# A two-layer hybrid decoder trunk on one core: all block sums of the MLP on VectorE, those of the last two channel pairs later, and the norm's sums issued further on

## The chip, the cores and the metric

The kernel runs on one core of a Trainium2 chip. A core has TensorE (PE, matrix products), VectorE (DVE), ScalarE (ACT), GpSimd (POOL) and SyncE (SP, which here only issues transfers). Each engine works through its own queue in order. The metric is the time of one execution in device microseconds, lower is better.

## The reference

Two layers over x of 1024 positions by 1024 channels, in float32. Each layer:

```
h = h + concat(pool_mixer(u), dilated_attention(q, k, v)) @ w_out      # from rmsnorm(h, norm1) @ w_in
hn = rmsnorm(h, norm2)
h = h + square(relu(hn @ w_up)) @ w_down                               # w_up 1024x4096, w_down 4096x1024
h = h + sigmoid(rmsnorm(h, norm3) @ w_gate) * (p[i] @ w_ple)
```

and a last rmsnorm. `rmsnorm(x, g) = x * rsqrt(mean(x*x) + eps) * g`, over the channels.

## The kernel before, in words

Activations are kept with channels on partitions, one tile of 128 channels by 1024 positions. The two products of the MLP are done by a scheme of seven products: the 2x2 block product of a pair of weight tiles with a pair of channel tiles and two halves of the positions takes seven products P1 to P7 of sums of blocks, in place of eight. So sums of blocks are needed on both sides. The sums of weights are made in `Seven.sums` (L305 to L319), four instructions per set of weights: `u0s` and `u1s` for the first product of layer 0 and 1 (w_up), `d0s` and `d1s` for the second (w_down). The sums of the activations that enter the second product are made in `Up.sums` (L1240 to L1263), four instructions `ys` per pair of channel tiles, after relu and square (`y`). Every block or sum that enters a product is split in two parts that TensorE takes at its fast rate: ScalarE makes the high part (L331, L1275), VectorE the rest (L333 for weights `u0p`, `d0p`; L1277 for activations `wP`). Each piece is thus three products of 128x512 for each of 4 channel pairs, 12 in all.

The first product (`Up`) has 16 sets, one per channel pair of the hidden layer; sets 0 and 1 go side by side, as do the last two, 14 and 15. Its results go to DRAM as `x_d`, seven blocks per pair, and come back one piece at a time (`x_back`, L1270). The second product (`Down`) has 16 steps of 7 pieces, 84 products each; a step takes 4 channel pairs into one pair of output tiles. Two steps use the same channel pairs, and it is in the second of the two that blocks for the steps to come are loaded. After a piece, VectorE adds its result into `acc` (L1294), and as P1, P6, P5 and P3 of a set share a bank of PSUM (X), P7 and P4 another (Z), the next piece of that bank begins when `acc` has read the one before.

The second norm's scale is needed at the gating after the first product's pieces (L1232), so its sums (`ss_b`, L469, eight column products that TensorE does in 16 records), its root and its broadcast by TensorE (`rb_b`, L494) are put among the first pieces of the first product. What is summed there, `sq_b`, is added up by GpSimd (L458) from squares that ScalarE makes.

The order of instructions is written by a planner, `Clock`: each strand of work is a generator that yields the ns until its next instruction, and the products move a clock of their own. Every engine's queue is filled in the order in which the clock comes to its strands. Tiles in SBUF are taken in turn from one pool of 49 blocks (`blk`); an instruction that takes a block up waits until the one that used it last has finished.

Before the change, `Seven.sums` runs on GpSimd throughout, and `Up.sums` on VectorE except for the last two pairs, 14 and 15 (`rush`), whose sums run on GpSimd at the start of the second product.

Of the kernel before, what the change touches and what calls it, by code (L numbers as in the profile page):

```python
# [117 lines left out]
def body(nc, tc, pools, A, out):  # L118
# [3 lines left out]
    def blk(name, dt=F32, shape=(128, 1024)):  # L122
        return sb.tile(list(shape), dt, name=name, tag="b")
# [102 lines left out]
    class Seven:  # L226
# [10 lines left out]
        def __init__(self, sets, seq, name, lead=(12, 6, 4), side=0):  # L237
            self.sets, self.seq, self.name = sets, seq, name
            load, sums, make = lead
            self.raw, self.sum, self.piece = {}, {}, {}  # L240
            self.first = {}
            self.begin, t = [], 0.0
            for q, (j, _) in enumerate(seq):
                self.first.setdefault(j, q)
                self.begin.append(t)
                t += 675.0 * sets[j][2]
            self.kicks = []
            for j, q in self.first.items():
                self.kick(q, load, lambda j=j: self.load(j))
                self.kick(q, sums, lambda j=j: ck.go(self.sums(j)))  # L250
            for q, (j, P) in enumerate(seq):
                fn = lambda j=j, P=P: ck.go(self.make(j, P), (name, j, P))
                if q < side:
                    self.kicks.append((-9000.0 + 1200.0 * q, fn))
                else:
                    self.kick(q, make, fn)
            self.kicks.sort(key=lambda x: x[0])
# [47 lines left out]
        def sums(self, j):  # L305
            a11, a12, a21, a22 = (self.block(j, t, k) for t in range(2) for k in range(2))
            n = self.sets[j][2]
            ss = self.two("s", n, (2, n, 128))
            s = [ss[0]()]
            add = nc.gpsimd.tensor_tensor  # L310
            self.sum[j] = s
            add(s[0][:, 0], a11, a21, op=OP.subtract)
            yield 1500.0
            add(s[0][:, 1], a21, a22, op=OP.add)
            yield 1500.0
            s.append(ss[1]())
            add(s[1][:, 0], s[0][:, 1], a11, op=OP.subtract)
            yield 1500.0
            add(s[1][:, 1], a12, s[1][:, 0], op=OP.subtract)  # L319
# [118 lines left out]
    class Norm:  # L438
# [8 lines left out]
        def add(self, src, hf):  # L447
            if self.sq is None:
                self.sq = blk(f"sq_{self.name}")
            if self.first[hf]:  # L450
                self.first[hf] = False
                nc.scalar.activation(self.sq[:, hs(hf)], src, AF.Square)
                self.n[hf] += 1
                return
            t = blk(f"sqt_{self.name}")
            nc.scalar.activation(t[:, :512], src, AF.Square)
            yield 700.0
            nc.gpsimd.tensor_tensor(self.sq[:, hs(hf)], self.sq[:, hs(hf)], t[:, :512], op=OP.add)  # L458
            self.n[hf] += 1
# [56 lines left out]
        def start(self, delay, after=None, sums=None, slack=900.0):  # L516
            def chain():
                yield from self.compact(range(8), sums)
                yield slack
                yield from self.bcast()  # L520
                yield 700.0
                if after:
                    after()
                    yield 2500.0
                self.done()
            ck.go(chain(), delay=delay)
# [96 lines left out]
    def layer(L, hT, norm, tabs):  # L623
# [445 lines left out]
        norm2 = Norm(f"b{L}")  # L1069
# [112 lines left out]
        outs = ws = w = None  # L1182


        norm2.start(17000.0, slack=3000.0)
        norm3 = None
        hg3 = {}
        PLACE = {"P1": 0, "P2": 1, "P3": 2, "P7": 3, "P5": 4, "P6": 5, "P4": 6}
# [16 lines left out]
        class Up(Set):  # L1205
# [34 lines left out]
            def sums(self, y):  # L1240

                d = x_d[self.j].rearrange("a p c -> p a c")
                if y is self.y2:
                    nc.sync.dma_start(out=d[:, 1:3], in_=y.rearrange("p (a c) -> p a c", a=2))
                    return
                nc.sync.dma_start(out=d[:, 0], in_=y[:, :512])
                rush = self.j >= n7 - 2
                if rush:
                    yield 6000.0
                sub = (nc.gpsimd if rush else nc.vector).tensor_tensor  # L1250
                slow = 1800.0 if rush else 700.0
                b11, b12, b21, b22 = y[:, :512], y[:, 512:], self.y2[:, :512], self.y2[:, 512:]
                s = [blk(f"ys{i}", F32, (128, 2, 512)) for i in range(2)]
                sub(s[0][:, 0], b22, b12, op=OP.subtract)
                yield slow
                sub(s[0][:, 1], b12, b11, op=OP.subtract)
                yield slow + 700.0
                sub(s[1][:, 0], b22, s[0][:, 1], op=OP.subtract)
                yield slow
                nc.sync.dma_start(out=d[:, 3:5], in_=s[0])  # L1260
                sub(s[1][:, 1], b21, s[1][:, 0], op=OP.subtract)
                yield 8000.0 if rush else 2000.0
                nc.sync.dma_start(out=d[:, 5:7], in_=s[1])  # L1263

        xw = [{} for _ in range(18)]
# [287 lines left out]
    for L in range(DEPTH):  # L1553
        hT, norm = layer(L, hT, norm, tabs if L == 0 else None)
        tabs = None
# [33 lines left out]
```

## Time and profile before

| | |
|---|---|
| time, median of 3 runs | 2304.93 us (2304.41 to 2306.55) |
| profiled execution | 2304.64 us, span 2302.9 us |
| PE busy | 2254.9 us (98%), 11088 records |
| DVE busy | 1684.2 us (73%) |
| ACT busy | 1012.7 us (44%) |
| POOL busy | 729.4 us (32%) |
| mean granted TensorE clock | 0.991 |

Times in the profile are microseconds from the span's start unless marked ns. A product of 128x512 on TensorE is listed with a length of about 390 ns, but the next one starts before it has ended; what counts is the distance from start to start. In rows that merge instructions (x12), the length is that from the first start to the last end. "idle before" is the time an engine stood still in front of an instruction, with the instruction whose end released it. Line numbers are those of the kernel before.

### The profile page before, as it was taken

What the parts mean: (1) busy time and instruction counts of PE and PEld (TensorE: products, weight loads), DVE (VectorE), ACT (ScalarE), POOL (GpSimd) and SP (SyncE); (2) the same over time, 40 slices, a digit from 0 to 9 for tenths busy, and PEclk for the clock granted to TensorE, in tenths of its full rate; (3) what the DMA queues carried; (4) which work ended last, traced back from release to release, by engine and by line L of the source; (5) the groups of instructions that cost most, each with busy time, mean ns of one, the idle gap of its engine ahead of it and who ended that gap; (6) DMA issues with size and microseconds to landing.
All of it is one profiled execution on the core that took longest, in us unless ns stands there. A gap on an engine that the chain in (4) does not pass through costs nothing.

```text
span 2302.9 us, 30834 instructions
## 1 busy us (share of the span) xinstructions
PE 2254.9 (98%) x11088; PEld 1859.6 (81%) x11088; DVE 1684.2 (73%) x2774; ACT 1012.7 (44%) x2147; POOL 729.4 (32%) x554
## 2 busy tenths in 40 slices
PE   8999999999998999999999999999999989999998
PEld 6887788788886888878887878878888868888888
DVE  7555767777779888896565467687777788888845
ACT  5244543433335344454324355344333453434645
POOL 5111126333335332342121122453332353233322
PEclk9999999999999999999999999999999999999999
DMA  6011143354448645431220122234445675546214
GB/s 183 19 48 20 38 111 99 106 172 154 152 143 286 201 129 174 147 115 46 61 60 19 38 48 73 76 101 151 151 151 165 210 239 150 170 133 179 78 57 136
DMA packets 296369, 275.65 MB, mean 120 GB/s; under 512 B 12476, under 2 KB 224056, under 8 KB 296216
## 3 DMA queue, kind: packets, MB, share of 16 engines
q1 hardware_dynamic: 293624, 270.04, 38.0%
q0 software_dynamic: 2272, 3.61, 0.9%
q8 instruction: 87, 1.43, 0.3%
q14 instruction: 66, 0.54, 0.1%
q10 hardware_dynamic: 320, 0.03, 0.0%
HBM read 200.99 MB, written 72.58 MB: 119 GB/s over the span
## 4 chain that ended last, share of the span: by engine, by line
PE 82%; DVE 9%; ACT 4%; POOL 3%; issue 2%; DMA 1%; SPq 0%; DVEq 0%; ACTq 0%; POOLq 0%
PE X L567 28%; PE Z L567 14%; PE Y L567 6%; PE in L552 5%; PE in L554 5%; PE in L550 5%; PE gt L554 3%; PE gt L552 3%; PE gt L550 2%; PE o L836 2%; PE s L785 2%; DVE wP L1277 1%; POOL res L1102 1%; PE e L817 1%; POOL sq_b L458 1%
## 5 line engine op out<-in xcount | busy, mean ns | idle before, releaser
L1277 DVE TENSOR_TENSOR wP<-wP 128x512 fp32r<-128x512 f32 x252 | 225.9, 920 | 1.7 <-ACT wP L1275 1.7
L567 PE MATMUL X<-wP,d1p 128*128 128x512 f32 x768 | 183.1, 394 | 10.1 <-DVE acc L1294 5.8
L567 PE MATMUL X<-wP,d0p 128*128 128x512 f32 x768 | 183.0, 394 | 10.1 <-DVE acc L1294 4.9
L567 PE MATMUL X<-xP,u0p 128*128 128x512 f32 x768 | 184.7, 393 | 0.0
L567 PE MATMUL X<-xP,u1p 128*128 128x512 f32 x768 | 184.5, 393 | 0.0
L567 PEld LDWEIGHTS X<-wP,d1p 128*128 128x128 f32 x768 | 145.2, 190 | 42.7 <-ACT wP L1275 5.7
L567 PEld LDWEIGHTS X<-wP,d0p 128*128 128x128 f32 x768 | 145.1, 190 | 42.6 <-ACT wP L1275 5.7
L567 PEld LDWEIGHTS X<-xP,u0p 128*128 128x128 f32 x768 | 145.8, 190 | 30.4
L567 PEld LDWEIGHTS X<-xP,u1p 128*128 128x128 f32 x768 | 145.6, 190 | 30.4
L1235 ACT ACTIVATE y<-y 128x1024 f32<-128x1024 f32 x64 | 67.5, 1055 | 219.7 <-DVE y L1232 219.7
L191 DVE SCALAR_TENSOR_TENSOR wl<-wr,gt,wh 128x128 fp32r<-128x128 f32 (+1 forms) x288 | 117.9, 441 | 44.4 <-ACT wh L197 44.1
L1275 ACT ACTIVATE wP<-wP 128x512 fp32r<-128x512 f32 x252 | 146.5, 617 | 3.1 <-DMA wP<-x_d 2.8
L680 POOL TENSOR_TENSOR rot<-rot,s 128x512 f32<-128x512 f32 x48 | 61.7, 1288 | 255.6 <-DVE rot L678 136.7
L804 ACT ACTIVATE sm<-sm,nm 128x128 f32<-128x128 f32 (+1 forms) x192 | 84.2, 440 | 79.9 <-DVE nm L801 77.6
L1294 DVE TENSOR_TENSOR acc<-acc,X 128x512 f32<-128x512 f32 x128 | 86.9, 679 | 35.0 <-PE X L567 34.7
L197 ACT ACTIVATE wh<-wr,gt 128x128 fp32r<-128x128 f32 (+1 forms) x304 | 101.8, 397 | 0.5 <-DMA wr<-in_w_in_dram 0.5
L567 PE MATMUL Z<-wP,d0p 128*128 128x512 f32 x384 | 92.7, 391 | 0.0
L567 PE MATMUL Z<-wP,d1p 128*128 128x512 f32 x384 | 92.4, 391 | 0.0
L567 PE MATMUL Z<-xP,u1p 128*128 128x512 f32 x384 | 91.6, 389 | 0.0
L567 PE MATMUL Z<-xP,u0p 128*128 128x512 f32 x384 | 91.6, 389 | 0.0
L567 PEld LDWEIGHTS Z<-wP,d0p 128*128 128x128 f32 x384 | 72.8, 190 | 15.3
L567 PEld LDWEIGHTS Z<-wP,d1p 128*128 128x128 f32 x384 | 72.6, 189 | 15.2
(478 smaller groups left out, 5864.8 us busy)
## 6 DMA issues: line engine op xcount, KB each, us to landing
wP<-x_d SPq DMA_DIRECT2D x252, 256.0 KB, 3.7
x_d<-ys SPq DMA_DIRECT2D x64, 512.0 KB, 3.7
wr<-in_w_in_dram SPq DMA_DIRECT2D x40, 512.0 KB, 4.7
u0r<-in_w_up_dram SPq DMA_DIRECT2D x32, 512.0 KB, 5.0
x_d<-y SPq DMA_DIRECT2D x32, 512.0 KB, 2.8
u1r<-in_w_up_dram SPq DMA_DIRECT2D x32, 512.0 KB, 5.2
d0r<-in_w_down_dram SPq DMA_DIRECT2D x28, 512.0 KB, 5.7
d1r<-in_w_down_dram SPq DMA_DIRECT2D x28, 512.0 KB, 5.2
```

Source lines behind the costliest of these rows:

```text
L191: nc.vector.scalar_tensor_tensor(l[:, k], raw[:, k], gs[k], f(h[:, k]), op0=OP.mult, op1=OP.subtract)
L197: nc.scalar.activation(h[:, k], raw[:, k], AF.Copy, scale=gs[k])
L550: nc.tensor.matmul(p, wh, h[:, cols], start=first and i == 0, stop=False)
L552: nc.tensor.matmul(p, wh, l[:, cols], start=False, stop=False)
L554: nc.tensor.matmul(p, wl, h[:, cols], start=False, stop=last and i == n - 1)
L567: nc.tensor.matmul(p, w[:, a, i], x[:, b], start=first and i == 0 and a == b == 0, stop=i == n - 1 and a == 1, skip_group_check=not first)
L680: nc.gpsimd.tensor_tensor(a, a, tb["s"][:, hs(hf)], op=OP.mult)
L804: nc.scalar.activation(self.sm[:, p, hh], self.sm[:, p, hh], AF.Exp, bias=nm[:, h:h + 1], scale=0.125, accum_out=ml[g][:, n, 4 + h:5 + h])
L1235: nc.scalar.activation(y, y, AF.Square)
L1275: nc.scalar.activation(t[:, 0], f(t[:, 1]), AF.Copy)
L1277: nc.vector.tensor_tensor(t[:, 1], f(t[:, 1]), f(t[:, 0]), op=OP.subtract)
L1294: nc.vector.tensor_tensor(a, a, p, op=OP.add)
```

## The change

Four edits. The weights' block sums of both products move from GpSimd to VectorE. The activations' block sums of the last two channel pairs move from GpSimd to VectorE too, and start 33000 ns of planned time after their `y` is stored in place of 6000; their own steps are 1500 ns in place of 1800, and the last transfer follows after 6000 in place of 8000. The norm's sums start at 25000 ns of planned time in place of 17000.

```diff
@@ Seven.sums
-            add = nc.gpsimd.tensor_tensor
+            add = nc.vector.tensor_tensor
@@ layer, ahead of the MLP
-        norm2.start(17000.0, slack=3000.0)
+        norm2.start(25000.0, slack=3000.0)
@@ Up.sums
                 rush = self.j >= n7 - 2
                 if rush:
-                    yield 6000.0
-                sub = (nc.gpsimd if rush else nc.vector).tensor_tensor
-                slow = 1800.0 if rush else 700.0
+                    yield 33000.0
+                sub = nc.vector.tensor_tensor
+                slow = 1500.0 if rush else 700.0
...
                 sub(s[1][:, 1], b21, s[1][:, 0], op=OP.subtract)
-                yield 8000.0 if rush else 2000.0
+                yield 6000.0 if rush else 2000.0
                 nc.sync.dma_start(out=d[:, 5:7], in_=s[1])
```

How the order of instructions moves, at three places. First TensorE's queue at the start of the first product of layer 0; `X_3762` and `X_3763` are the banks of sets 0 and 1, `xP` the activations' pieces, `ss_b` the norm's sums. Before the change it reads:

```order
L567 MATMUL X_3762<-xP_3620,u0p 128x512 x3
L567 MATMUL X_3762<-xP_3828,u0p 128x512
L469 MATMUL ss_b_3926<-one,sq_b_3153 128x1 x8
L567 MATMUL X_3762<-xP_3828,u0p 128x512 x2
L567 MATMUL X_3763<-xP_3282,u0p 128x512 x3
```

Now the norm's sums have these rows around them:

```order
L567 MATMUL X_3763<-xP_3455,u0p 128x512 x3
L567 MATMUL X_3763<-xP_3627,u0p 128x512 x3
L567 MATMUL X_3763<-xP_3864,u0p 128x512
L469 MATMUL ss_b_3984<-one,sq_b_3153 128x1 x8
L567 MATMUL X_3763<-xP_3864,u0p 128x512 x2
L567 MATMUL Z_3860<-xP_3303,u0p 128x512 x3
```

The sums stand 36 products further on, near the end of the fifth piece of sets 0 and 1 (P5) in place of inside the fourth (P6); `rb_b` follows 27 products behind them, as against 27 before.

Second, VectorE's queue at the start of the second product of layer 0, around the first `acc`; `d0r` are raw weights, `d0s` their sums, `d0p` the split pieces. Before the change it reads:

```order
L1277 TENSOR_TENSOR wP_6098<-wP_6098 128x512
L1294 TENSOR_TENSOR acc_0_6039<-acc_0_6039,X_6149 128x512
L333 TENSOR_TENSOR d0p<-d0r_5964,d0p 128x512
L1277 TENSOR_TENSOR wP_6111<-wP_6111 128x512
L1277 TENSOR_TENSOR wP_6126<-wP_6126 128x512
```

Now the first `acc` has these rows around it:

```order
L314 TENSOR_TENSOR d0s_6145<-d0r_6088 128x512
L1277 TENSOR_TENSOR wP_6098<-wP_6098 128x512
L1294 TENSOR_TENSOR acc_0_6039<-acc_0_6039,X_6149 128x512
L317 TENSOR_TENSOR d0s_6182<-d0s_6145,d0r_6086 128x512
L333 TENSOR_TENSOR d0p<-d0r_5964,d0p 128x512
L1277 TENSOR_TENSOR wP_6111<-wP_6111 128x512
L319 TENSOR_TENSOR d0s_6182<-d0r_6086,d0s_6182 128x512
L1277 TENSOR_TENSOR wP_6126<-wP_6126 128x512
```

The sums of the next step's weights come between the pieces of this one. From the `y<-y,Y` that stands at 698.91 in the trace up to the first `acc` of the second step's first piece there are 55 instructions before and 63 now.

Third, VectorE's queue from the second into the third step; `ys` are the sums of pairs 14 and 15, made of `y`, and `acc_0_6399` belongs to the third step. Now it reads:

```order
L1294 TENSOR_TENSOR acc_0_6251<-acc_0_6251,X_6298 128x512
L1256 TENSOR_TENSOR ys_6442<-y_5817 128x512
L333 TENSOR_TENSOR d0p<-d0s_6339,d0p 128x512
L1277 TENSOR_TENSOR wP_6393<-wP_6393 128x512
L1254 TENSOR_TENSOR ys_6471<-y_5888,y_5840 128x512
L1277 TENSOR_TENSOR wP_6397<-wP_6397 128x512
L1258 TENSOR_TENSOR ys_6443<-y_5865,ys_6442 128x512
L1294 TENSOR_TENSOR acc_0_6399<-acc_0_6399,X_6458 128x512
L312 TENSOR_TENSOR d0s_6484<-d0r_6403,d0r_6405 128x512
```

Before the change, between the same two `acc`:

```order
L1294 TENSOR_TENSOR acc_0_6258<-acc_0_6258,X_6312 128x512
L333 TENSOR_TENSOR d0p<-d0s_6354,d0p 128x512
L1277 TENSOR_TENSOR wP_6409<-wP_6409 128x512
L1277 TENSOR_TENSOR wP_6413<-wP_6413 128x512
L1294 TENSOR_TENSOR acc_0_6415<-acc_0_6415,X_6471 128x512
```

Three `ys` come between the two `acc`, and the first `d0s` of a later step behind the second. Over the stretch from the split piece ahead of these rows to the `acc` that the trace before has at 782.01, there are 23 instructions before and 35 now.

## Rows read from the trace of the kernel before

**Rows 1.** The table of stretches, the four that hold a loss and one that holds none (us from the span's start; then length, and for each engine in the order PE, PEld, DVE, ACT, POOL its busy us and the instructions counted; granted clock, DMA share, GB/s).
```profile
400.00:500.00 100.00, 95.10 (x413) 78.41 (x412) 76.39 (x100) 44.54 (x74) 31.85 (x21) 0.95 0.42 137
...
700.00:800.00 100.00, 91.55 (x389) 74.51 (x388) 88.36 (x108) 43.61 (x76) 45.17 (x28) 0.97 0.72 233
800.00:900.00 100.00, 100.00 (x443) 82.84 (x442) 87.55 (x114) 42.66 (x76) 32.87 (x22) 1.00 0.50 148
...
1500.00:1600.00 100.00, 95.28 (x414) 78.61 (x413) 76.44 (x94) 40.46 (x67) 47.80 (x30) 0.95 0.37 116
...
1800.00:1900.00 100.00, 91.51 (x389) 74.56 (x388) 83.20 (x102) 49.25 (x86) 39.54 (x26) 0.97 0.74 242
```

**Rows 2.** The list of waits, TensorE alone (who waits for whom: us in total, times, longest).
```profile
PE X L567 <- DVE acc L1294: 10.7, 5, 3.4
PE ss_b L469 <- POOL sq_b L458: 9.5, 4, 3.2
...
PE X L567 <- DVE d0p L333: 4.3, 2, 3.6
PE X L567 <- DVE d1p L333: 4.3, 2, 3.6
```

**Rows 3.** The timeline of all engines around the norm's sums in the first layer (start, length, engine, line, operation, tiles, count, and in brackets the idle time before it and what ended it).
```profile
411.71 5.60 PE L567 MATMUL Z<-xP,u0p 128*128 128x512 f32 x24
...
417.15 2.43 PE L567 MATMUL X<-xP,u0p 128*128 128x512 f32 x10
...
421.17 4.88 POOL L458 TENSOR_TENSOR sq_b<-sq_b,sqt_b 128x512 f32<-128x512 f32 x3 [0.74 <-ACT sqt_b L456]
...
422.77 1.69 PE L469 MATMUL ss_b<-one,sq_b 128*128 128x1 f32 x8 [3.19 <-POOL sq_b L458]
...
426.11 1.86 PE L469 MATMUL ss_b<-one,sq_b 128*128 128x1 f32 x8 [1.66 <-POOL sq_b L458]
...
427.84 8.94 PE L567 MATMUL X<-xP,u0p 128*128 128x512 f32 x27
...
432.62 0.17 DVE L485 TENSOR_TENSOR r_b<-r_b,q_b 128x8 f32<-128x8 f32 x1
...
436.61 0.60 PE L494 MATMUL rb_b<-cst,r_b 128*128 128x128 f32 x4
```

**Rows 4.** The timeline of TensorE where the third norm's sums are made, the same operation without a wait.
```profile
1046.88 1.84 PE L469 MATMUL ss_c<-one,sq_c 128*128 128x1 f32 x16
1048.59 0.48 PE L552 MATMUL gt<-g_0L,wh 128*128 128x512 f32 x1
```

**Rows 5.** The table of stretches of 10 us (columns as in rows 1).
```profile
420.00:430.00 10.00, 5.58 (x21) 5.11 (x22) 4.14 (x5) 4.60 (x9) 8.50 (x7) 0.65 0.35 102
...
1020.00:1030.00 10.00, 9.26 (x40) 7.22 (x40) 10.00 (x13) 4.49 (x8) 4.40 (x4) 1.00 0.22 72
```

**Rows 6.** The timeline of TensorE where the second product begins, first layer.
```profile
717.75 0.61 PE L567 MATMUL X<-wP,d0p 128*128 128x512 f32 x2
721.95 3.46 PE L567 MATMUL X<-wP,d0p 128*128 128x512 f32 x10 [3.58 <-DVE d0p L333]
...
730.35 3.00 PE L567 MATMUL X<-wP,d0p 128*128 128x512 f32 x12 [1.49 <-DVE acc L1294]
...
747.61 4.42 PE L567 MATMUL X<-wP,d0p 128*128 128x512 f32 x12 [3.37 <-DVE acc L1294]
751.87 2.90 PE L567 MATMUL Z<-wP,d0p 128*128 128x512 f32 x12
```

**Rows 7.** The timeline of VectorE in the same place, from the last instruction that waited for TensorE to the sum that is level with it again.
```profile
698.91 0.69 DVE L1217 TENSOR_TENSOR y<-y,Y 128x512 f32<-128x512 f32 x1 [0.28 <-PE Y L567]
...
711.76 1.28 DVE L1277 TENSOR_TENSOR wP<-wP 128x512 fp32r<-128x512 f32 x2
...
738.33 1.78 DVE L333 TENSOR_TENSOR d0p<-d0s,d0p 128x512 fp32r<-128x512 f32 x1
...
748.46 0.67 DVE L1294 TENSOR_TENSOR acc<-acc,X 128x512 f32<-128x512 f32 x1
```

**Rows 8.** The timeline of GpSimd beside the third row of the group before.
```profile
737.82 1.74 POOL L1256 TENSOR_TENSOR ys<-y 128x512 f32<-128x512 f32 x1
```

**Rows 9.** The list of instruction groups, VectorE (count | busy us, mean ns of one | idle before).
```profile
L1277 DVE TENSOR_TENSOR wP<-wP 128x512 fp32r<-128x512 f32 x252 | 225.9, 920 | 1.7 <-ACT wP L1275 1.7
...
L1294 DVE TENSOR_TENSOR acc<-acc,X 128x512 f32<-128x512 f32 x128 | 86.9, 679 | 35.0 <-PE X L567 34.7
```

**Rows 10.** The timeline of VectorE in the first product: the wide gating step with GpSimd idle.
```profile
658.84 1.22 DVE L1232 SCALAR_TENSOR_TENSOR y<-y,rs_b 128x1024 f32<-128x1024 f32 x1
```

**Rows 11.** The timeline of VectorE in the second and third step of the second product.
```profile
763.57 0.69 DVE L333 TENSOR_TENSOR d0p<-d0s,d0p 128x512 fp32r<-128x512 f32 x1
...
770.98 0.67 DVE L1294 TENSOR_TENSOR acc<-acc,X 128x512 f32<-128x512 f32 x1
...
782.01 0.69 DVE L1294 TENSOR_TENSOR acc<-acc,Z 128x512 f32<-128x512 f32 x1 [0.74 <-PE Z L567]
```

**Rows 12.** The timeline of TensorE beside it: the product that takes up Z again.
```profile
779.09 2.88 PE L567 MATMUL Z<-wP,d0p 128*128 128x512 f32 x12
```

**Rows 13.** The timeline of GpSimd there.
```profile
764.10 1.30 POOL L312 TENSOR_TENSOR d0s<-d0r,d0r 128x512 f32<-128x512 f32 x1 [12.73 <-DMA d0r<-in_w_down_dram]
```

**Rows 14.** The timeline of TensorE near the end of the second product.
```profile
1020.96 5.44 PE L567 MATMUL X<-wP,d0p 128*128 128x512 f32 x22 [0.74 <-DVE d0p L333]
```
## The prediction, made before the result was known

> **What bounds the kernel now.** I read the table of stretches first, then the list of TensorE's waits, then the timelines of the places they name. TensorE is the bound: a stretch without trouble is busy for 100.00 us of 100 and holds 443 products; four stretches fall short, two in each layer, with 413, 389, 414 and 389 [rows 1]. VectorE, at 76 to 88 us of 100, is the next busiest and GpSimd stands far below it. The waits have two names only: the norm's sums `ss_b` wait 9.5 us for GpSimd's last squares, and `X` waits for VectorE's `acc`, `d0p` and `d1p` [rows 2]. The layers are alike to one product of 400 [rows 1], so I work out one and double it.
>
> At full clock a product of 128x512 starts every (417.15 - 411.71) / 24 = 0.2267 us [rows 3]. That is the yardstick for what each place costs.
>
> *The norm.* Ten products start at 417.15 and so end their turn at 419.42. The next ordinary product starts at 427.84, 8.42 us later; the 16 little products of `ss_b` are between. Unhindered they take 1048.59 - 1046.88 = 1.71 us [rows 4], so 6.71 us are lost. The wait (3.19 + 1.66 us) is most of it; the rest is the clock, granted at a mean of 0.65 in the stretch of the wait [rows 5]: of the engine's levels, 1.2 GHz for part of it, 2.4 before. The 27 products behind it take 436.61 - 427.84 = 8.77 us where 27 x 0.2267 = 6.12 would do: 2.65 us more. Together 9.4 us.
>
> *The start of the second product.* From 717.75 to 751.87 TensorE starts eight pieces of 12, that is 96 products, in 34.12 us [rows 6]; at full clock they take 21.76. 12.4 us are lost, 8.44 of them waits (3.58 + 1.49 + 3.37) and the rest low clock. All three waits end with VectorE, which has no idle time worth the name from 698.91, where it last waited for TensorE, to 748.46 [rows 7]. Between these two starts stand 55 of its instructions, 53 narrow (128x512) and 2 wide (128x1024). Alone, narrow ones follow each other every 0.60 us (two of them take 1.28, and one takes 0.68) [rows 7] and a wide one takes 1.22 [rows 10]: 53 x 0.60 + 2 x 1.22 = 34.2 us. They took 49.55. The other 15.3 us are stretched instructions: `d0p` at 738.33 takes 1.78 and ends 0.55 us after GpSimd's sum of 737.82, which runs to 739.56 [rows 7, 8]. The groups say the same: `wP`, both inputs in SBUF, averages 920 ns, `acc`, which reads PSUM, 679 [rows 9].
>
> The Trainium skill (page "SBUF — State Buffer", section "Who interferes with whom") states this as a lock: an instruction of VectorE with two SBUF inputs and one of GpSimd that reads SBUF exclude each other for a whole instruction. The rows agree. By that rule, all 15.3 us go when GpSimd stops summing, as the sum below has it.
>
> **The change, part by part.**
>
> *A, the norm's sums issued later.* `ss_b` moves behind 36 more products on TensorE. They last 36 x 0.2267 = 8.2 us, so it stands at 419.42 + 8.2 = 427.6; GpSimd's last sum of squares ends at 421.17 + 4.88 = 426.05 [rows 3], 1.5 us before. The wait goes, and the low clock with it. Next in the chain is the broadcast `rb_b`, now 27 products behind `ss_b`: 427.6 + 1.7 + 6.1 = 435.4. Its scale was ready at 432.62 + 0.17, that is 4.95 us after `ss_b` ended; 4.95 after 429.3 is 434.3, early enough. The little products stay. Bounds: from 9.4 us saved to about half of that if the margin of 1.5 us is used up. I take 9.4.
>
> *B, the block sums at the start of the second product.* In the same stretch VectorE now has 63 instructions, 61 narrow and 2 wide: the eight sums `d0s` come in (4.8 us), the eight sums `ys` are not among them, and GpSimd stands idle. 61 x 0.60 + 2 x 1.22 = 39.0 us, so VectorE is through at 698.91 + 39.0 = 737.9. TensorE cannot ask earlier: the sum at the end is that of the seventh piece, which ends at 717.75 + 84 x 0.2267 = 736.8 at best. VectorE is 1.1 us too slow, which shows as one wait of some 1.2 us at the third piece, since `acc` must empty X before that piece adds to it. A wait of 0.74 us left the clock at 1.00 [rows 5, 14], and I count none for the clock. 12.4 - 1.2 = 11.2 us saved. Bounds: 12.4 if VectorE starts ahead; nothing if the stretching is not GpSimd's.
>
> Here a price of the Trainium skill weighs against the change (page "VectorE: DVE Perf Modes", section on the TRN2 errata): an fp32 tensor_tensor of 512 takes 691 ns. By it, as an estimate, the 61 would take 42.2 us, the wait would be 5.6 us longer in each layer, and the time 2280. The row decides for 0.60, as the second of two starts before the first has ended [rows 7].
>
> *C, the sums `ys` of the last two channel pairs, 33 us later.* They now stand on VectorE from the last pieces of the second step into the third. From 763.57 to 782.01, 18.44 us [rows 11], VectorE got through 23 instructions; in the new order 35 stand there (eight `ys`, four `d0s`), 21.0 us. It falls up to 2.6 us behind. The first sum with no room is the 27th: 763.57 + 26 x 0.60 + 0.69 = 779.9, where TensorE takes up Z again at 779.09 [rows 12]: 0.8 us of wait at least. Between 0.8 and 2.6 I take 1.7 us lost per layer. Behind the waiting product nothing but TensorE's own queue suffers. The lag is made up in the next step, which has fewer loads.
>
> *D, transfers.* The four blocks of `y` stay in SBUF longer, so loads that take up blocks in turn start later, and SP's queue now meets the transfers of `ys` among the third step's loads. No row shows a price; bounds are 0 and the longest load wait shown, 12.73 us [rows 13], and I take 1 us per layer, near the low end, because the pieces those loads feed lie a step ahead.
>
> *E, the sums in the rest of both products.* Four sums in every step of 84 products (19.04 us) are 2.4 us, 13% of VectorE. Beside 87.55 us of 100 [rows 1] that would be too much, if the stretching stayed; 126 `wP` a layer at 920 instead of 680 ns alone [rows 9] give back 30 us in the 16 steps of 19.04, or 10%. I count E at nothing: TensorE loses nothing there now [rows 1] and VectorE is left no fuller.
>
> Sum per layer: -9.4 - 11.2 + 1.7 + 1.0 = -17.9 us. The profiled execution took 2304.64 us (span 2302.9), 0.3 below the median of 2304.93. 2304.6 - 35.8 = **2268.8 us**.
>
> **Rivals.**
> - *VectorE stays the bound where the second product starts.* B and C bring nothing, A alone: 2304.6 - 18.8 = 2286. For it: VectorE gets eight instructions more there. Against: 15.3 us of stretching. Chance 0.12.
> - *The second step overflows.* The wait of C is the whole 2.6 us and the clock falls as behind the wait of 3.37, where 12 products took 4.26 us instead of 2.72 [rows 6]; the loads of D cost 2 us. 2.6 + 1.5 + 2.0 = 6.1 instead of 2.7: 2269 + 7 = 2276. For it: a step with loads is full already. Chance 0.2.
> - *An added instruction costs its length, 0.68, not its step.* B ends 61 x 0.08 = 4.9 us later per layer: 2279. Chance 0.05.
> - *`ss_b` still waits,* because the squares end over 1.5 us later: half of A, 2278. Chance 0.06.
> - *Slower: a sum stops VectorE's queue.* On GpSimd a sum that waited for a load or a block stopped nothing else; on VectorE `acc` and the pieces stand behind it. The longest such wait is 12.73 us, for a load that let the sum go at 764.10 [rows 13]. In the new order that sum stands behind the `acc` of 770.98 [rows 11], 6.9 us later. If loads slip by more than that at a few steps of each layer, waits of this size return on the engine that TensorE needs: four of them are 51 us, 2269 + 51 = 2320. It decides from 36 us in all. Chance 0.04.
>
> **How the numbers follow.** The forecast keeps 0.53; its own range is 2262 (C and D nothing, B nearly whole) to 2275. The rivals above it lie at 2276 to 2286, so the range is 2261 to 2284. What the measurement tells from no change is 0.2%, 4.6 us: every case but the last is faster than that, and I leave 0.02 for a gain lost on the way. Faster 0.94, same 0.02, slower 0.04.
>
> **What would show it.** In the changed profile `ss_b` has no wait for GpSimd and its stretch a clock of 1.00 (A). `wP` falls from 920 ns to about 680, and TensorE's waits for `acc`, `d0p` and `d1p`, 19.3 us over both layers, to a few (B). A short wait of Z or X for `acc` some 10 us into the third step is C. Waits of VectorE for a load or for a product in front of the block sums, with TensorE waiting behind them, would make it wrong; so would `wP` still at 900.

## The result, and the profile after

The changed kernel takes 2268.53 us (median of 4 runs, 2268.15 to 2269.02) beside 2304.85 us for the kernel before: ratio 0.9841, 95% interval 0.9824 to 0.9858. The forecast was 2268.8 us. The profiled execution took 2269.02 us, its span is 2267.2.

The page's first part (busy us, share of the span, instructions):

```profile
PE 2240.3 (99%) x11088; PEld 1849.0 (82%) x11088; DVE 1643.2 (72%) x3046; ACT 1011.6 (45%) x2147; POOL 313.9 (14%) x282
```

The 272 sums have moved from GpSimd (554 instructions before) to VectorE (2774 before). VectorE does them and is still busy for 41 us less than the 1684.2 before.

The table of stretches, which answers to [rows 1]:

```profile
400.00:500.00 100.00, 100.00 (x453) 82.81 (x452) 80.02 (x124) 44.76 (x74) 6.33 (x4) 1.00 0.43 137
...
700.00:800.00 100.00, 97.35 (x429) 79.95 (x428) 91.25 (x149) 48.34 (x84) 0.00 (x0) 1.00 0.74 229
800.00:900.00 100.00, 100.00 (x443) 82.81 (x442) 79.20 (x128) 41.48 (x73) 0.00 (x0) 1.00 0.52 155
...
1500.00:1600.00 100.00, 100.00 (x454) 82.81 (x453) 83.03 (x129) 45.32 (x75) 6.81 (x5) 1.00 0.43 137
...
1800.00:1900.00 100.00, 97.35 (x429) 79.94 (x428) 90.41 (x147) 50.37 (x88) 0.00 (x0) 1.00 0.82 261
```

The norm's stretches are full, at a clock of 1.00. The starts of the second product have 429 products in place of 389, where a full stretch has 443.

The list of TensorE's waits, for [rows 2]:

```profile
PE X L567 <- DVE acc L1294: 5.0, 4, 1.6
...
PE Z L567 <- DVE acc L1294: 2.0, 2, 1.0
...
PE X L567 <- DVE d1p L333: 0.7, 1, 0.7
PE X L567 <- DVE d0p L333: 0.7, 1, 0.7
```

`ss_b` is no longer in it. TensorE's timeline at the two places and at the third step, layer 0, for [rows 3, 6, 12]:

```profile
417.92 10.59 PE L567 MATMUL X<-xP,u0p 128*128 128x512 f32 x46
428.35 1.84 PE L469 MATMUL ss_b<-one,sq_b 128*128 128x1 f32 x16
...
709.24 2.88 PE L567 MATMUL X<-wP,d0p 128*128 128x512 f32 x12
...
716.47 3.01 PE L567 MATMUL X<-wP,d0p 128*128 128x512 f32 x12 [1.63 <-DVE acc L1294]
...
732.92 2.88 PE L567 MATMUL Z<-wP,d0p 128*128 128x512 f32 x12
...
757.40 2.88 PE L567 MATMUL Y<-wP,d0p 128*128 128x512 f32 x12
761.29 3.03 PE L567 MATMUL Z<-wP,d0p 128*128 128x512 f32 x12 [1.02 <-DVE acc L1294]
764.16 8.32 PE L567 MATMUL X<-wP,d0p 128*128 128x512 f32 x36
```

The sixteen little products of `ss_b` stand at 428.35 in one run of 1.84 us, without a wait. Where eight pieces took 34.12 us before, they now go from 709.24 to 732.92, 23.68 us. Two waits are left in each layer at the places that the prediction named: one at the third piece and one some ten microseconds into the third step. The other two of the list, 0.87 us at an `acc` and 0.74 at a split piece, stand near the end of the second product, and did so before the change.

VectorE's timeline from the `y<-y,Y` that waits for TensorE to the `acc` of the seventh piece, and its groups, for [rows 7, 9]:

```profile
690.40 0.69 DVE L1217 TENSOR_TENSOR y<-y,Y 128x512 f32<-128x512 f32 x1 [0.28 <-PE Y L567]
...
710.83 0.69 DVE L1277 TENSOR_TENSOR wP<-wP 128x512 fp32r<-128x512 f32 x1
711.43 0.69 DVE L312 TENSOR_TENSOR d0s<-d0r,d0r 128x512 f32<-128x512 f32 x1
712.03 0.69 DVE L1277 TENSOR_TENSOR wP<-wP 128x512 fp32r<-128x512 f32 x1
...
715.64 0.68 DVE L1294 TENSOR_TENSOR acc<-acc,X 128x512 f32<-128x512 f32 x1
...
730.40 0.69 DVE L1294 TENSOR_TENSOR acc<-acc,X 128x512 f32<-128x512 f32 x1 [0.85 <-PE X L567]
```

```profile
L1277 DVE TENSOR_TENSOR wP<-wP 128x512 fp32r<-128x512 f32 x252 | 171.0, 697 | 0.9 <-ACT wP L1275 0.9
L1294 DVE TENSOR_TENSOR acc<-acc,X 128x512 f32<-128x512 f32 x128 | 87.4, 683 | 55.6 <-PE X L567 55.6
```

Instructions follow each other every 0.60 us without a gap (711.43 - 710.83, 712.03 - 711.43), and `wP` has nearly the length of `acc`, a mean of 697 ns against 920 before. From 690.40 to 730.40 stand the 63 instructions of the prediction's sum; less the 0.85 us that VectorE waits for TensorE at the end they take 39.15 us, where 39.0 were forecast and 55 took 49.55 before.

By TensorE's timelines, the time of each product of the MLP before and after (us):

| | layer 0 | layer 1 | forecast |
|---|---|---|---|
| first product, start to start of the second | 316.92 to 307.64: -9.28 | 316.68 to 307.63: -9.05 | A: -9.4 |
| second product, start to first gating product | 319.36 to 310.26: -9.10 | 319.22 to 310.24: -8.98 | B + C + D: -8.5 |

Together that is 36.4 us; the spans differ by 35.7, since the first product of layer 0 begins 0.77 later.

### The profile page after: what moved, and what is told of

Same layout as the page of the kernel before. It is cut to its first block, busy times and chain, and to the rows that moved or that the text cites. A ratio compares the mean times of both kernels' runs of the same rounds, so it can differ in the third digit from the quotient of the medians.

```text
span 2267.2 us, 30544 instructions
## 1 busy us (share of the span) xinstructions
PE 2240.3 (99%) x11088; PEld 1849.0 (82%) x11088; DVE 1643.2 (72%) x3046; ACT 1011.6 (45%) x2147; POOL 313.9 (14%) x282
## 3 DMA queue, kind: packets, MB, share of 16 engines
q8 instruction: 87, 1.43, 0.3%
## 4 chain that ended last, share of the span: by engine, by line
PE 91%; DVE 5%; DMA 1%; ACT 1%; issue 1%; POOL 1%; SPq 0%; DVEq 0%; ACTq 0%
PE X L567 29%; PE Z L567 14%; PE Y L567 7%; PE in L552 5%; PE in L554 5%; PE in L550 5%; PE gt L554 3%; PE gt L552 3%; PE gt L550 3%; PE po L552 2%; PE po L550 2%; PE po L578 2%; PE po L554 2%; PE o L836 2%; PE s L785 2%
## 5 line engine op out<-in xcount | busy, mean ns | idle before, releaser
L458 POOL TENSOR_TENSOR sq_c<-sq_c,sqt_c 128x512 f32<-128x512 f32 x28 | 41.8, 1496 | 1162.0 <-ACT sqt_c L456 1161.1
L1277 DVE TENSOR_TENSOR wP<-wP 128x512 fp32r<-128x512 f32 x252 | 171.0, 697 | 0.9 <-ACT wP L1275 0.9
```

The source lines that it names most:

```text
L1277: nc.vector.tensor_tensor(t[:, 1], f(t[:, 1]), f(t[:, 0]), op=OP.subtract)
```

## The experiments

Each kernel ran beside the kernel before on the same chip. "Before" and "after" mean the two kernels of the change. Where two changed kernels differ by a few microseconds, the lengths of the two products in their traces, taken as in the table above, tell more than the ratios.

### Are the norm and the sums two separate gains?

*norm_alone*: before, with one edit.

```diff
-        norm2.start(17000.0, slack=3000.0)
+        norm2.start(25000.0, slack=3000.0)
```

> Before, with the norm's sums at 25000 ns and nothing else changed. My theory (A is a loss of its own, 9.4 us a layer, and does not need VectorE relieved): 2304.85 - 18.8 = 2286 us; ss_b has no wait for GpSimd, the stretch from 400 to 500 us holds a clock of 1.00, and TensorE's waits for acc, d0p and d1p stay at some 19 us. Rival (what the norm gives is lost again at the start of the second product, where VectorE is the bound): 2300 us or more, with longer waits there.

Measured: 2293.48 us, ratio 0.9949 (0.9934 to 0.9964). `ss_b` waits for nothing and the clock of the stretch is 1.00, as expected, but only 11.0 us are gained, not 18.8. The rival is not it: the second product takes 319.80 us in layer 0, where it took 319.36. TensorE stops just in front of the norm's new place, for ScalarE, which empties the bank X. Its timeline, and under it those of ScalarE, VectorE and GpSimd:

```profile
424.70 5.29 PE L567 MATMUL X<-xP,u0p 128*128 128x512 f32 x22 [2.01 <-ACT y L1214]
```

```profile
409.41 0.73 ACT L1088 ACTIVATE xP<-res,gt 128x512 fp32r<-128x512 f32 x1 [2.89 <-DVE res L1126]
...
424.05 0.59 ACT L1214 ACTIVATE y<-X 128x512 f32<-128x512 f32 x1
```

```profile
387.95 1.78 DVE L1153 SCALAR_TENSOR_TENSOR t<-res,gt,t 128x512 f32<-128x512 f32 x1
...
402.15 0.68 DVE L1124 TENSOR_TENSOR res<-po,h_6H 128x512 f32<-128x512 f32 x1
```

```profile
387.44 1.74 POOL L312 TENSOR_TENSOR u0s<-u0r,u0r 128x512 f32<-128x512 f32 x1
```

Three of the four rows of ScalarE and VectorE as they stand in the kernel after:

```profile
407.27 0.73 ACT L1088 ACTIVATE xP<-res,gt 128x512 fp32r<-128x512 f32 x1 [2.89 <-DVE res L1126]
```

```profile
388.71 0.74 DVE L1153 SCALAR_TENSOR_TENSOR t<-res,gt,t 128x512 f32<-128x512 f32 x1
...
400.03 0.68 DVE L1124 TENSOR_TENSOR res<-po,h_6H 128x512 f32<-128x512 f32 x1
```

The fourth, `y<-X`, stands at 421.91 there. With the norm's edit alone ScalarE is 2.14 us later in both rows, VectorE 2.12 at `res`: GpSimd's weight sums ahead of the first product (`u0s`) stretch VectorE, ScalarE waits for VectorE and is late with the bank. The first product takes 400.77 to 710.70, 309.93 us: 6.99 gained, not 9.28. The trace is of an execution of 2291.45 us, 13.2 us under the trace of the kernel before; what the other three, of 2293 to 2294 us, lose besides is not shown.

*sums_alone*: after, with the norm's sums back.

```diff
-        norm2.start(25000.0, slack=3000.0)
+        norm2.start(17000.0, slack=3000.0)
```

> After, with the norm's sums back at 17000 ns. My theory: the wait for the squares is there again in each layer, some 4 us and the low clock behind it, so 7.5 to 9.4 us a layer and 2284 to 2287 us; the waits for acc, d0p, d1p stay as in after. Rival (with GpSimd free of the weights' sums the squares are added early enough by themselves, and the move of the norm's sums was not needed): 2269 to 2275 us.

Measured: 2280.15 us, ratio 0.9892 (0.9877 to 0.9907), between the two expectations. TensorE's timeline:

```profile
420.03 1.05 PE L469 MATMUL ss_b<-one,sq_b 128*128 128x1 f32 x8 [0.38 <-POOL sq_b L458]
423.37 1.86 PE L469 MATMUL ss_b<-one,sq_b 128*128 128x1 f32 x8 [2.29 <-POOL sq_b L458]
425.10 7.97 PE L567 MATMUL X<-xP,u0p 128*128 128x512 f32 x27
```

The wait is 2.67 us where it was 4.85, for the same reason: GpSimd's last sum of squares ends at 423.32 in place of 426.05, as VectorE and ScalarE are earlier. So the sums alone already win 3.80 and 2.72 us of the first product's loss in the two layers. The norm's edit is worth 11.6 us on top of the sums and 11.0 without them; the sums are worth 24.4 to 25, where the prediction's B, C and D had 17.0. Each place's loss was sized rightly, but the losses of the first product do not belong to the norm's edit alone.

### What stretched VectorE's instructions?

*idle_sums* and *idle_memsets*: after, with work on GpSimd that nothing waits for, in the weights' sums of the second product; VectorE's and TensorE's queues are those of after.

```diff
@@ tiles
+    ghost = small.tile([128, 384], F32, name="ghost", bufs=1)
@@ Seven.sums
+            if self.name[0] == "d" and j < 4:
+                nc.gpsimd.tensor_tensor(ghost[:, :4], a11[:, 0, :4], a21[:, 0, :4], op=OP.subtract)
+                gv = ghost.rearrange("p (i c) -> p i c", i=3)
+                for _ in range(12):
+                    nc.gpsimd.tensor_tensor(gv, a11[:, :3], a21[:, :3], op=OP.subtract)
```

In *idle_memsets* the last line is `nc.gpsimd.memset(gv, 0.0)`. Line numbers behind these additions are 6 higher in both.

> After, with work added on GpSimd that nothing waits for: behind the loads of each of the first four sets of w_down in a layer, 12 subtractions of 128x384 from the raw weights into a scratch tile. VectorE's and TensorE's queues are those of after. My theory (GpSimd's reads of SBUF stretch VectorE's instructions with two inputs in SBUF, about 0.5 us for each us): some 50 us of GpSimd a layer, VectorE 20 us later or more where it has no room, wP and d0p again 1.2 to 1.8 us long beside them, acc unchanged at 0.68; TensorE waits 12 to 25 us more a layer, 2295 to 2318 us. Rival (the engines do not hinder each other, the stretching before had to do with the order or with data that came late): 2268.5 us.

> As idle_sums, with each of the 12 subtractions replaced by a memset of the same scratch tile, which reads nothing (one small subtraction per set is left to start them in the same place). My theory (it is GpSimd's reading that hinders): VectorE's instructions keep 0.68, 2268.5 to 2270 us. Rival (any work of GpSimd in SBUF hinders): longer instructions of VectorE here too, and a time between this and that of idle_sums.

Measured: idle_sums 2330.93 us, ratio 1.0112 (1.0095 to 1.0129); idle_memsets 2268.46 us, ratio 0.9842 (0.9827 to 0.9857). GpSimd's timeline in idle_sums, then VectorE's, then the same two in idle_memsets:

```profile
709.16 18.14 POOL L317 TENSOR_TENSOR ghost<-d0r,d0r 128x384 f32<-128x384 f32 x12
742.52 0.20 POOL L314 TENSOR_TENSOR ghost<-d0r,d0r 128x4 f32<-128x4 f32 x1 [15.22 <-DMA d0r<-in_w_down_dram]
742.80 16.84 POOL L317 TENSOR_TENSOR ghost<-d0r,d0r 128x384 f32<-128x384 f32 x12
```

```profile
724.89 1.51 DVE L1283 TENSOR_TENSOR wP<-wP 128x512 fp32r<-128x512 f32 x1
...
730.78 0.68 DVE L1283 TENSOR_TENSOR wP<-wP 128x512 fp32r<-128x512 f32 x1
...
745.73 1.52 DVE L1283 TENSOR_TENSOR wP<-wP 128x512 fp32r<-128x512 f32 x1
747.17 0.67 DVE L1300 TENSOR_TENSOR acc<-acc,X 128x512 f32<-128x512 f32 x1
```

```profile
704.87 5.66 POOL L317 MEMSET ghost<- 128x384 f32 x12
```

```profile
709.40 0.68 DVE L339 TENSOR_TENSOR d0p<-d0s,d0p 128x512 fp32r<-128x512 f32 x1
```

`wP` takes 0.9 to 1.5 us as long as GpSimd sums, the shorter ones right behind an instruction with an input in PSUM, and 0.68 in the pause from 727.3 to 742.5; `acc`, with one input in PSUM, keeps 0.67 in the midst of it. The stretches say the same: from 691 to 727 VectorE gets through 33 instructions in 36 us, from 727 to 742 through 24 in 15. That is the stretching of the kernel before, made by sums that no one waits for. The size was underestimated (2295 to 2318): GpSimd's 48 subtractions took 68.8 us a layer (1.43 each), not 50, and the granted clock, at a mean of 0.81 from 691 to 727, fell behind TensorE's waits. The memsets take 5.66 us for 12, and VectorE's nine instructions beside them keep 0.68 (1.22 the wide one), the lengths of after. They occupy GpSimd for only a third of the time that 12 subtractions take, but in that time nothing is stretched.

*weights_on_vectore*: before with the norm's edit and the weights' sums on VectorE; `ys` of the last two pairs stays on GpSimd, at 6000 ns.

```diff
-            add = nc.gpsimd.tensor_tensor
+            add = nc.vector.tensor_tensor
...
-        norm2.start(17000.0, slack=3000.0)
+        norm2.start(25000.0, slack=3000.0)
```

> Before with the norm moved and the weights' sums on VectorE; the sums ys of the last two pairs stay on GpSimd, at once. VectorE has the same number of instructions at the start of the second product as in after, but GpSimd still sums for some 13 us there. My theory (stretched instructions, about 0.5 us of VectorE for each us of GpSimd): VectorE 6.6 us later, the loss C of after gone, 2268.5 + 2 x (6.6 - 1.3) = 2279 us, wP still long beside each ys. Rival (the gain of B is a matter of how the instructions stand, not of GpSimd): 2266 us, without C.

Measured: 2283.58 us, ratio 0.9907 (0.9893 to 0.9922). VectorE's timeline in front of the first `acc`:

```profile
713.19 1.19 DVE L333 TENSOR_TENSOR d0p<-d0s,d0p 128x512 fp32r<-128x512 f32 x1
714.30 1.76 DVE L333 TENSOR_TENSOR d0p<-d0r,d0p 128x512 fp32r<-128x512 f32 x1
715.99 1.75 DVE L314 TENSOR_TENSOR d0s<-d0r 128x512 f32<-128x512 f32 x1
...
718.26 0.68 DVE L1294 TENSOR_TENSOR acc<-acc,X 128x512 f32<-128x512 f32 x1
```

Three instructions beside three `ys` of GpSimd put this `acc` 2.62 us later than in after (718.26 against 715.64). TensorE waits 4.30 us for it, and 1.98 for a later one, with the granted clock down behind both (0.79 from 720 to 730, 0.89 from 730 to 740). The forecast, 2279, was too low by 4.6 us; it had no term for the clock. (For the first the list names a `wP` of ScalarE that ends at the same moment; but `acc` ends at 718.94 and the product starts 0.15 later, as it does in after, at 716.32 and 716.47.) The rival, the order alone, would have given 2266. So two pairs' sums, 16 instructions in the whole kernel, make 15 us. Two things about them differ from after: the engine, with the planner's steps that go with it, and the place, 6000 ns in place of 33000. *ys_at_once*, below, has them on VectorE at the early place and takes 2275.38 us. Some 8 of the 15 us thus go with the engine, although VectorE has eight instructions more in each layer there, and 7 with the place. Where GpSimd sums counts for more than how much.

### Where may `ys` stand?

Three kernels are after with one number changed.

```diff
-                    yield 33000.0
+                    yield 6000.0
```

> After, with the sums ys of the last two pairs on VectorE at once (6000 ns) in place of 33000. My theory (VectorE is the bound at the start of the second product, each instruction 0.60 us): eight more, 4.8 us, of which a part is taken up by VectorE's idle time at 729 to 745; C's 1.3 us goes. 2268.5 + 2 x (4.8 - 1.3) = 2275.5 us, with the waits at acc of the first step. Rival (it is the late blocks and loads that cost, and VectorE has room): 2265 us.

> After, with the sums ys at 20000 ns in place of 33000: they stand in the second half of the first step and the second step's beginning, where VectorE of after is idle for 3.8 us between 729 and 745 and eight ys need 4.8. My theory (C is VectorE's lack of room around 745 to 761 and nothing else): the wait of 1.02 us at Z goes, TensorE waits for VectorE by less than 0.5 us there, 2268.5 - 2 x 1.2 = 2266 us. Rival (the eight have no room here either): new waits of 1 to 2 us a layer at acc or wP, 2268 to 2271 us.

> After, with the sums ys at 52000 ns: in the third step, where VectorE of after is idle for 4.7 us between 769 and 789. The blocks of y are held 19 us longer. My theory (C is VectorE's room alone, and D, the blocks held, costs nothing): the wait at Z goes, 2266 us. Rival (blocks held too long stop the loads of the second step, D): TensorE waits for d0p or wP behind late loads, 2270 us or more.

| `ys` at | time, us | ratio to before (95%) | TensorE's waits at these places, layer 0 |
|---|---|---|---|
| 6000 ns | 2275.38 | 0.9874 (0.9857 to 0.9890) | 1.64 `acc`, 0.97 `wP`, 2.32 (see below) |
| 20000 ns | 2266.13 | 0.9834 (0.9820 to 0.9847) | 1.63 `acc` |
| 33000 ns (after) | 2268.53 | 0.9841 (0.9824 to 0.9858) | 1.63 `acc`, 1.02 `acc` |
| 52000 ns | 2273.91 | 0.9865 (0.9852 to 0.9879) | 1.63, 1.82 and 0.69 `acc` |

At 6000 the sums push VectorE back by 0.60 us each, and the time is the one forecast. The list puts the wait of 2.32 us down to a `wP` of ScalarE; but `acc` ends 0.15 us before that product starts (733.64 and 733.79), the distance that the two keep in after, so this wait too is for `acc`. At 20000 the sums fall into VectorE's idle time and the wait of C is gone, with the 2.4 us that it was priced at. The ratios of 20000 and 33000 ns overlap, but the second product takes 308.97 and 308.90 us in the two layers in place of 310.26 and 310.24. At 52000 something else happens. VectorE's timeline there, and ScalarE's:

```profile
765.47 0.69 DVE L333 TENSOR_TENSOR d0p<-d0s,d0p 128x512 fp32r<-128x512 f32 x1 [4.87 <-ACT d0p L331]
766.08 0.68 DVE L1294 TENSOR_TENSOR acc<-acc,Z 128x512 f32<-128x512 f32 x1
```

```profile
764.80 1.31 ACT L331 ACTIVATE d0p<-d0s 128x512 fp32r<-128x512 f32 x2 [9.11 <-PE X L567]
```

ScalarE waits 9.11 us for a product of TensorE to end before it may write a `d0p`; its source, the `d0s`, has been ready since 755.79. What the product releases is, as far as the program tells, the block that this `d0p` takes up, since `y` still holds four; no run with a larger pool shows it. VectorE, in order, stands still for 4.87 us behind that piece, and `acc` behind VectorE. This is the mechanism of the slower rival, with a split piece in place of a sum, and of term D. The rival of the forecast had late loads in this role. In the kernel after it does not occur: from 754 to 800 ScalarE waits 4.21 us at most for a product, VectorE never waits for ScalarE, and apart from waits for TensorE (1.43 us at most) it has only this one, for a load.

```profile
770.68 0.69 DVE L312 TENSOR_TENSOR d0s<-d0r,d0r 128x512 f32<-128x512 f32 x1 [0.19 <-DMA d0r<-in_w_down_dram]
```

### What is left of B?

*d_sums_5_ahead* and *d_sums_4_ahead*: after, with the middle number of the second product's lead (loads, sums, pieces) at 5 or 4.

```diff
-        D7 = Seven(sevens[L][1], seq2, f"d{L}", (9, 6, 3))
+        D7 = Seven(sevens[L][1], seq2, f"d{L}", (9, 5, 3))
```

> After, with the second product's weight sums begun 5 pieces ahead in place of 6 (2.7 us later): two sums fewer stand in front of the first acc. My theory (what is left of B is VectorE's number of instructions in front of that acc, 0.60 us each): the wait of 1.63 us at the third piece falls to some 0.4, 2268.5 - 2.4 = 2266 us. Rival (the wait is set by ScalarE's pieces or by TensorE): the wait stays, 2268.5 us.

> After, with the second product's weight sums begun 4 pieces ahead: again two sums fewer in front of the first acc (none of the four of the second set stands there), so the third piece waits as with 5; but the sums come 5.4 us later than in after, and a split piece of them may be late. My theory: 2266 us as with 5, unless TensorE waits for d0p at the first pieces made of sums; in that case 1 us a layer is lost again, 2268 us.

Measured: 2270.17 us (0.9849, 0.9836 to 0.9863) and 2274.85 us (0.9869, 0.9855 to 0.9882). The third piece waits 0.84 and 1.02 us in place of 1.63, so the instructions in front of `acc` count, though by less than 1.2 us: with two sums fewer VectorE waits 0.45 us for a `wP` of ScalarE ahead of that `acc`, as it does not in after, so the rival has a part in it. But the sums came later everywhere, and the last steps lost more, 2.02 and 3.25 us at one `acc` where after waits 0.87. Both expectations had left those steps out. With 5 the executions lie from 2268.43 to 2271.68 us, and the second product of layer 0 takes 310.31 us, as in after (310.26): the one gain is used up by the other loss.

*places_7_ahead* and *places_8_ahead* combine what had helped: `ys` at 20000, and the lead changed for three sets only (the edit to the lead, shown with 8; line numbers behind it are 1 higher).

```diff
-                self.kick(q, sums, lambda j=j: ck.go(self.sums(j)))
+                n = {1: 5}.get(j, 8 if j >= len(sets) - 2 else sums) if name[0] == "d" else sums
+                self.kick(q, n, lambda j=j: ck.go(self.sums(j)))
```

> After, with three places set anew: ys at 20000 ns, the second set's weight sums of the second product 5 pieces ahead (one piece later than in after), those of the last two sets 7 ahead (one piece earlier). From ys_20us 2266.1, less 0.8 us a layer at the third piece, as d_sums_5_ahead showed, less up to 0.87 us a layer at the last steps, where one piece later cost 1.15 more: 2262.8 us. Rival (one of the waits only moves to the next piece): 2264.5 to 2266 us.

> As places_7_ahead with the last two sets' sums 8 pieces ahead. My theory: the wait of 0.87 us at the last steps is gone at 7 already or goes here, 2262.5 us. Rival (the earlier sums crowd VectorE a piece before): a wait of some 1 us there, 2264 us or more.

Measured: 2266.18 us (0.9832, 0.9817 to 0.9846) and 2265.77 us (0.9830, 0.9815 to 0.9844), little or nothing below ys_20us, as the rivals had it. The third piece waits 0.96 us and 0.24 more at a `wP`; the 0.87 us at the last steps stays in both. VectorE's and TensorE's timelines of places_8_ahead there:

```profile
974.55 0.69 DVE L1295 TENSOR_TENSOR acc<-acc,X 128x512 f32<-128x512 f32 x1 [0.83 <-PE X L568]
```

```profile
971.64 2.88 PE L568 MATMUL X<-wP,d0p 128*128 128x512 f32 x12
975.39 4.82 PE L568 MATMUL X<-wP,d0p 128*128 128x512 f32 x20 [0.87 <-DVE acc L1295]
```

VectorE itself had been waiting for the piece before (it ends at 971.64 + 2.88 = 974.52), and the next piece needs that very `acc`. So no order of the sums shortens this wait, which is the same 0.87 us in the kernel before. The best kernel of the study is so 2265.8 us, 0.1% below the change, and all but 0.4 us of that is `ys` at 20000.

## Why the prediction was right, and where it was not

- *What bounds the kernel* held. TensorE's losses stood at the two places of each layer, and their sizes (9.4 and 12.4 us) are what the change could win; 9.2 and 10.4 were won.
- *A* was sized rightly as a place and wrongly as an edit. The step "the wait goes, and the low clock with it" gave all 9.4 us to the norm's move. The first product gained 9.28 and 9.05 us, but norm_alone gained 6.99: the other 2.3 came from VectorE being free of GpSimd ahead of the first product. The prediction takes no row from there, though the trace before has `L1153` at 1.78 us in it (387.96). That the sum for the place came out all the same is luck: the change happened to hold both edits. The margin was better than forecast for the same reason: GpSimd's last sum ends at 424.01 and `ss_b` starts at 428.35, 4.3 us in place of 1.5.
- *B* was right in kind. The rule of the Trainium skill on two SBUF inputs (page "SBUF — State Buffer", section "Who interferes with whom"), that VectorE with two SBUF inputs and a reading GpSimd exclude each other, and that one that only writes does not, is borne out by idle_sums and idle_memsets. VectorE's 39.0 us are there (39.15), but eight pieces lose 23.68 - 21.76 = 1.9 us, not 1.2. The step that failed is where the lag was taken: at the seventh piece, when it shows at the third, with six of the eight new sums in front of the first `acc`. At the seventh VectorE is through and waits 0.85 us for TensorE. 10.4 us gained, not 11.2.
- *The price of an instruction*, 0.60 us by the row, is what VectorE's queue shows: 0.68 to 0.69 long, started every 0.60. The rival that took the length fails on it. The Trainium skill's 691 ns (page "VectorE: DVE Perf Modes", section on the TRN2 errata) agree with the length and are not the price.
- *C* is there at its place, 761.29 where 760.12 was due and 0.15 more behind, 1.3 us against 1.7.
- *D* is nothing at 33000 ns; the 1.0 us, a guess between wide bounds, was too much. Blocks held too long do cost at 52000, if the reading there is right, by a split piece and not by a load.
- *E* is nothing: the stretches between hold 443 products as before, with VectorE no fuller.

The sum per layer, -9.2 - 10.4 + 1.3 + 0 = -18.3 against -17.9 forecast, comes out so close because small misses of both signs cancel (B 0.8 us short, D 1.0 too dear). The rival on VectorE as the bound fails by the waits that are left, the overflow of the second step by the 1.02 us there, and `ss_b` does not wait. The slower rival is not in this kernel; 19 us of planned time further on its kind of stop appears, 4.87 us of VectorE's queue, and costs 5.4 us in all, not 51.

## What to carry to other kernels

When VectorE's instructions with two SBUF inputs come at two lengths (0.68 and 1.2 to 1.8 us here), look at what GpSimd does beside them before counting instructions: work moved onto the busier engine can leave it less busy. Price a moved instruction by the step of a full queue, and look for room with the engine's idle time in the timeline; when it holds tiles of a shared pool, ask who takes the next one. And attribute a loss to an edit only after following the chain of the other engines into that place.

## What the runs showed of the hardware

- GpSimd pays too. In the kernel before its 128x512 sum takes 1.26 us at 426.02, where VectorE stands idle, and 1.74 beside VectorE's `d0p` [rows 8]. In idle_memsets 12 memsets of 128x384 take 5.66 us, 0.47 each, and stretch none of VectorE's instructions beside them.
- The clock behind a wait of about 2 us is not settled by the length of the wait. In d_sums_5_ahead the same wait of 2.02 us is followed by 36 products in 8.42 us in layer 0, with a granted clock of 1.00, and by 36 in 10.03 us in layer 1, with a mean of 0.83 over the 10 us around their start (shown below). In ys_52us 12 products take 4.57 us after a wait of 1.82; in after, 3.01 after 1.63. What separates them stays open.

```profile
977.00 8.42 PE L567 MATMUL X<-wP,d0p 128*128 128x512 f32 x36 [2.02 <-DVE acc L1294]
...
2088.97 10.03 PE L567 MATMUL X<-wP,d1p 128*128 128x512 f32 x36 [2.02 <-DVE acc L1294]
```
